# A two-layer decoder trunk in fp32 halves on one core: the weights' low halves all subtracted on VectorE, none on GpSimd, with a new issue order

## The chip, the cores and the metric

One core of one Trainium2 chip. The time is the device time of one execution in microseconds; the figure for a kernel is the median of its runs. TensorE (PE) multiplies, VectorE (DVE), ScalarE (ACT) and GpSimd (POOL) work on tiles in SBUF and PSUM, and SyncE (SP) issues the loads. Each engine takes its own instructions strictly in the order in which the program issues them.

## What is computed

Two decoder layers on 256 positions of width 1024, all in fp32. Per layer:

```python
h = rms_norm(x, pre_mix_norm[i]); z = h @ w_in[i]             # 1024 -> 2560, four head groups
out_a = block attention; out_b = gMLP spatial gating
out_c = conformer convolution (31 taps, depthwise); out_d = differential attention
x = x + rms_norm(concat(out_a, out_b, out_c, out_d) @ w_out[i], post_mix_norm[i])
x = x + rms_norm(gated conv FFN(rms_norm(x)), post_ffn_norm[i])  # up 1024 -> 5632, down 2816 -> 1024
x = x + sigmoid(rms_norm(x) @ w_pe_gate[i]) * (p[i] @ w_pe_proj[i])
```

## The kernel before, in words

**Weights in halves.** A matmul of fp32 accuracy is made of three in a reduced format (`mm3`): high times high, high times low, low times high. So each weight needs a rounded high part and the rest. All weights are packed into pieces of 128 x 2048 and loaded as halves of 128 x 1024, numbered k = 0 to 207 in the order of use (`PIECES`, `need`). `prep(k)` (line 303) gives each half three tiles of one ring of 25 (`TAGS`, tag `wt`): `raw` (512 KB, loaded by SP), `hi` (a rounding copy on ScalarE) and `lo` (raw minus hi). Which engine subtracts is read from a list, `POOL` (line 32), of 68 of the 206 halves that go through `prep`:

```python
nc.scalar.activation(hi, raw, AF.Copy)
eng = nc.gpsimd if k in POOL else nc.vector
eng.tensor_tensor(lo, raw, hi.bitcast(F32), op=ALU.subtract)
```

Both inputs of this subtraction lie in SBUF. The two halves of the first piece are made from four smaller loads (`rq`, `hq`, `lq`).

**The stages.** A layer is a mixer (`mixer`, line 483), a feed-forward part (`ffn`, line 889) and a gate. In the mixer TensorE projects `ca`, `cg`, `b`, `dk`, `dq`, `v`, `ak`, `aq`; VectorE rotates the queries and keys (`rot_*`), adds 60 convolution taps (`cacc`, one input in PSUM), makes the scaled, masked scores and their minima (`ed`, `ea`), layer norms (`gv`, `bl_ln`), the lambda of the differential attention (`lam_j`) and the low parts of each group's output (`cat_lo`); ScalarE makes exponentials and the high parts. Each group's output is then multiplied by its rows of `w_out` into the four tiles `y000` to `y011`. After the post norm the transposed rows become `hf_hi` and `hf_lo`. In the feed-forward part 22 tiles `u` are made by 48 matmuls each, each passing through VectorE (`u`, `uc`, `f`) and ScalarE, and 22 steps of the down projection (`f000` to `f011`) take them up. GpSimd also makes small reciprocal roots (`*_v`, `*_r`), masks and constants.

**The order of the work.** The program first records all operations (`Prog.record`), then issues them in the order that a long string, `ORDER` (line 1075), spells out (`Prog.issue`, line 190). A token is the engine's letter (t, v, s, g; s also stands for the loads of SyncE) and the tile: `v.lo20` is the subtraction of half 20 on VectorE, `t.dq0*28` the next 28 matmuls into `dq0`, `v.cacc0@5` the sixth tap. A tile gets a place of its ring when it is first issued, and gives it back after its last use. The string had been made by a planner outside the kernel. At the start TensorE runs 28 transposes that nothing uses (`busy`, `WARM`).

Of the kernel before, what the change touches and what calls it, by code (L numbers as in the profile page):

```python
# [1075 lines left out]
g.nhalf g.mask g.ident s.xt1 g.ident t.busy*2 g.ones t.busy*15 s.gc s.h0_hi@2 s.xt0 s.h0_hi@1 s.h0_hi*2 s.xt3 s.rq3  # L1076
s.rq0 g.mask s.xt2 s.rq2 v.h0_lo@1 s.posi s.h0_hi@6 v.h0_lo v.h0_lo@3 v.h0_lo@6 s.h0_hi@7 s.hq3 s.fr s.hq0 s.raw4
v.h0_lo v.h0_lo@7 v.lq3 v.lq0 s.h0_hi@5 v.h0_lo@5 t.busy s.rq1 t.ca0 s.h0_hi v.h0_lo s.raw2 s.hq2 v.lq2 s.hi4 s.xs
g.posf s.hq1 g.ang@2 s.hi2 s.xs@2*2 s.xs s.raw5 s.raw3 s.raw7 s.cols0 s.raw8 s.raw6 s.raw13 s.raw26 s.x10_s t.ca0*9
t.busy*8 t.ca0*4 t.busy*2 t.b00 v.lo4 t.b00*2 s.raw32 s.raw11 v.lq1 t.b00 t.ca0*24 s.raw9 s.raw10 t.ca0 t.cg0*2  # L1080
t.ca0*9 g.ang g.kf@2 g.kf v.lo2 g.kf s.x00_s s.x11_s g.n01_v s.x01_s g.n00_v g.n01_r g.n00_r s.hi5 t.cg0 g.kf t.cg0*3
s.hi3 v.lo3 t.cg0*22 v.lo5 s.mr0_d t.mr0 s.mr0_d s.hi7 t.mr0 t.cg0*6 v.ang@4 v.ang v.ang@5 t.cg0 v.ang t.cg0*7 s.hi8
t.cg0*6 t.b00*2 v.ang@6 s.mr0 v.ca0 v.cg0 s.hi6 g.cols0*2 v.lo6 t.b00*6 v.ang@7 v.ang s.cth g.ang@3 s.sin_d v.cg0
v.lo7 s.cacc0@1 s.cacc0 s.cos_d*2 s.hi9 t.b00*7 t.b01*10 t.b00*3 s.pt0 t.b00 s.raw20 s.raw17 s.raw12 v.ang s.hi13
g.ang s.raw14 s.raw19 v.cacc0@1 v.cacc0 s.chalf t.b00 g.lo8 s.raw29 s.gv s.raw15 s.raw24 v.cacc0@3 v.cacc0 v.cacc0@5
v.cacc0 v.cacc0@7 v.cacc0 v.cacc0@9 v.cacc0 v.cacc0@11 g.cos_d v.cacc0 s.gu v.cacc0@13 v.cacc0 v.cacc0@15 v.cacc0
t.b01*7 s.hi10 t.b01*5 s.raw18 t.b01*2 s.gu t.dk0*6 g.lo9 t.dk0*14 s.gv t.dk0*28 t.dq0 g.lo10 t.dq0*19 s.hi11 g.lo11
s.hi12 g.lo12 s.hi14 g.lo13 s.raw16 s.ph0 s.sin_a t.dq0*4 s.hi17 v.cacc0@17 v.cacc0 v.cacc0@19 v.tab_d0 v.cacc0@21
v.tab_d0 v.cacc0@23 v.cacc0 v.cacc0@25 s.hi19 v.cacc0 v.cacc0@27 v.cacc0 v.cacc0@29 v.rot_dk0 v.cacc0@31 v.dk0
v.cacc0@33 v.dk0 v.bl01_st t.dq0*23 v.cacc0 v.cacc0@35 v.rot_dk0 s.cos_a*2 s.hi16 s.hi29 s.first v.cacc0 v.bl01_mv  # L1090
g.lo14 t.dq0 v.rot_dq0 v.cacc0 v.dq0 v.cacc0 v.dq0 s.hi15 v.cacc0@37 v.cacc0 v.rot_dq0 t.v00*18 t.sc013 t.sc011
t.sc002 t.sc013 v.cacc0 v.bl00_st v.cacc0@39 g.bl01_v g.lo17 g.lo15 g.bl01_r v.bl00_mv v.ed03@2 t.sc011 s.sd1_0@6
v.ed01@3 t.sc002 v.ed02@1 s.raw27 v.ed02 v.ed03@3 s.sd1_0@7 t.v01*2 v.cacc0 t.v01*5 s.sd0_0@3 g.bl00_v v.ed01@2
v.cacc0 v.cacc0@41 v.cacc0 v.cacc0@43 t.v01*3 v.cacc0 t.sc001 t.sc010 t.sc003 t.sc010 t.sc003 s.raw28 v.ed03 v.cacc0
t.sc001 v.ed01@1 v.ed01 t.v01 t.v00*6 t.v01*2 s.hi27 t.v01*4 t.sc012 s.hi28 s.raw23 v.ed03 s.hi23 s.vsb00 g.lo16
t.sc000 t.sc012 t.sc000 g.bl00_r v.cacc0@46 v.cacc0 s.sd0_0@2 v.ed00@2 v.cacc0@48 s.hi18 s.sd1_0@2 v.ed00@3 s.sd1_0@1
s.sd1_0@4 s.sd1_0@3 s.sd1_0 t.v01*6 s.sd1_0 t.v01 v.lo19 s.rows0 v.lam_w v.gv*2 v.lam_w s.lam_w s.vsb01 v.bl0_ln*2
s.sd0_0@4 v.ed00 t.ak0 s.sd0_0 g.cos_a t.ak0*5 v.rd1_0@1 t.ak0*7 v.rd1_0 t.ak0*13 s.raw21 v.cacc0@50 v.cacc0
v.tab_a0@1 v.tab_a0 g.lo18 v.ed00 s.hi24 v.ed02 s.sd0_0 v.ed02 t.bm0*3 s.sd0_0@6 s.sd0_0*2 v.nlam0 t.bm0 v.bo v.cacc0
v.bo v.cd0 s.hi20 v.cd0 s.hi21 v.ed02 v.ed02@6*2 v.ed00@6 v.ed00 s.raw45 v.ed00*2 t.ak0*5 s.br00_s t.ak0 t.aq0*2  # L1100
t.ak0*3 v.ed02 t.ak0*2 t.aq0*15 s.g_post_mix0 t.aq0*3 t.ak0*11 t.wd00_pt s.br01_s t.aq0 t.wd00_pt*2 t.aq0*2 v.cacc0@52
t.aq0*3 s.hi26 t.aq0*5 s.raw22 v.rd0_0 v.rot_ak0 v.cacc0 v.ak0 v.cacc0@54 g.br00_v g.br01_v s.wd00_ps g.br00_r
s.br00_o t.wd00_pt t.aq0 t.wd00_pt g.br01_r t.wd00_pt s.br01_o s.od0*2 v.ak0 t.bt0*3 s.raw25 t.bt0 t.aq0*3 g.gsub0
t.aq0*13 t.wd03_pt*3 v.cacc0 v.rot_ak0 s.cat0_hi@1 s.cat0_hi v.cat0_lo*2 v.rot_aq0 v.rd0_0 v.aq0 v.cacc0@56 v.aq0
g.lo20 t.y000*3 t.wd02_pt*3 s.hi22 t.y000 s.wd03_ps t.wd03_pt*3 s.wd02_ps t.y001 t.wd02_pt*3 v.cacc0 v.rot_aq0 v.cacc0
s.od0@7 v.cacc0 s.od0@6 s.od0@4 g.lo21 g.lo26 t.y001 t.wd01_pt s.hi32 t.y001*2 t.y000*2 s.od0@5 t.wd01_pt*2 s.wd01_ps
t.sca03 v.cacc0 t.sca00*2 v.ea00 t.sca03 t.ct0*2 v.ea00 t.ct0*2 v.cst@1 v.cmv@1 g.cl01_v s.sa0*2 v.ea03@1 v.ra0 v.cst
v.cmv v.ea03 t.wd01_pt*3 s.od0@3 s.od0 g.cl01_r t.y011 v.cnm@1 t.y011*5 g.cl00_v g.cl00_r t.wa00_pt*3 t.y001*2 s.odsq
v.odss t.sca01 v.cnm s.wa00_ps t.sca02 t.sca01 v.ea01 t.sca02 g.odv g.odr t.wa00_pt*3 s.cn@1 v.ea02 s.cn t.csT0 v.ea02
t.csT0*2 s.oa0@1 s.oa0 v.ea01 t.csT0 s.cth2@1 s.cth2 s.cs t.y010*2 s.cs v.od0 v.cs*2 v.lo22 t.y010*4 t.pj001 t.pj010  # L1110
s.sa0@4 t.dt0*4 s.cat0_hi@3 t.cp0*4 v.co@1 v.co s.cat0_hi t.y010 t.y011 t.y000*2 s.sa0@6 v.cat0_lo@3 s.sa0@5 t.y011
s.raw36 v.cat0_lo v.ra0@2 s.sa0*3 s.cr00_s g.cr00_v t.wa03_pt*2 v.ra0@3 t.wa03_pt s.wa03_ps s.cr01_s t.y001*3 v.ra0
t.wa02_pt*3 s.wa02_ps t.y010 t.wa03_pt*3 t.y000*2 g.cr00_r g.cr01_v g.cr01_r v.lo23 s.oa0*2 s.cr00_o t.wa02_pt*3
v.lo27 t.wa01_pt*3 t.y011*2 t.y010*2 s.cr01_o s.wa01_ps t.wa01_pt*2 s.oa0@5 s.oa0 t.wa01_pt s.oa0 s.ar00_s g.ar00_v
g.ar00_r t.y001 t.y010 t.ctt0*4 s.oa0 s.cat0_hi v.cat0_lo s.ar01_s g.ar01_v t.y011 g.ar01_r t.y000*2 t.y001 t.y011
t.y001*2 t.y000 t.y001*2 t.y000 s.cat0_hi v.cat0_lo s.ar00_o v.lo28 s.raw30 v.pl0 s.raw33 t.y001 t.at0 v.lo29 t.y001
s.ar01_o t.at0 s.raw31 t.at0*2 s.cat0_hi*2 t.y010*3 s.raw47 s.hi30 s.raw39 t.y000*2 s.hi25 v.cat0_lo t.y001 t.y000*3
v.cat0_lo v.lo24 t.y000 t.y001 v.lo32 t.y001*5 s.pm001_s t.y000*4 s.pm000_s g.pm00_v g.pm00_r t.y010 t.y011*12 s.hi33
s.hi31 v.y000 v.xs t.nf00_t@1 t.nf00_t s.pm00x0_s v.y001 v.xs s.hf0_hi v.hf0_lo t.y010 s.pm011_s t.y010*4 t.pj001
s.hf0_hi g.lo25 v.hf0_lo s.raw42 t.y010 s.pm00x1_s v.y011 g.nf00_v s.raw37 t.nf00_t s.hf0_hi t.y010 v.hf0_lo t.y010*2  # L1120
t.nf00_t t.pj001*3 s.hf0_hi v.hf0_lo s.pm010_s t.pj001 s.proj001 t.nf00_t s.hf0_hi t.nf00_t s.hf0_hi t.pj010*5
s.proj010 v.y010 t.pj011*2 v.hf0_lo t.nf00_t s.hf0_hi g.nf00_r v.hf0_lo t.nf00_t t.pj011*3 s.hf0_hi t.pj000 g.pm01_v
g.pm01_r v.xs s.pm01x0_s v.hf0_lo*2 t.nf01_t s.hf0_hi v.hf0_lo t.pj011 t.nf01_t t.pj000*4 g.lo30 s.hf0_hi v.hf0_lo
s.proj011 t.nf01_t t.pj000 t.nf01_t t.u00*6 s.hf0_hi t.u00 v.xs v.hf0_lo s.hf0_hi v.hf0_lo s.proj000 t.nf01_t t.u00
g.lo31 t.nf01_t s.hf0_hi v.hf0_lo s.hf0_hi v.hf0_lo s.pm01x1_s s.qr0_d t.u00*3 t.u01*5 g.nf01_v t.u01 t.nf01_t
s.hf0_hi v.hf0_lo t.nf01_t s.hf0_hi s.hi36 s.hi39 s.raw38 v.hf0_lo s.hi38 g.nf01_r s.qr0_d v.lo33 v.lo36 s.raw34
s.hi34 t.u00*29 t.u01 t.u00*2 t.u01 t.qr0*2 t.u00*6 s.raw43 s.raw48 s.raw51 v.lo39 s.qr0 s.hi43 g.lo34 t.u01*4 s.raw35
t.u01*8 v.u00 s.uc0*2 s.raw49 t.u01*10 v.uc0@1 t.u01 v.uc0@3 v.uc0*2 s.raw40 s.hi37 g.lo37 s.uc0 s.raw44 t.u01*17
v.u01 t.u02*5 s.hi51 t.u02*23 v.lo38 s.uc1@1 v.uc0 s.uc1 v.uc1*3 s.hi47 v.uc1 s.hi44 v.lo44 t.u02*13 s.hi42 t.u02*6
t.u03*5 t.u02 t.u03*11 v.u02 s.uc2 g.lo42 v.uc2 v.uc2@2 s.uc2 v.uc2*2 s.hi45 t.u03*11 v.lo45 t.u03*21 s.f0 s.raw55  # L1130
# [192 lines left out]
```

## Time and profile before

| | us |
|---|---|
| median of 3 runs | 662.68 (662.63, 662.68, 665.95) |
| the profiled execution | 666.75 |
| its span, first to last instruction | 665.0 |
| TensorE busy | 645.8 |
| VectorE busy | 498.3 |
| ScalarE busy | 429.3 |
| GpSimd busy | 218.3 |

The span is the time from the first to the last instruction on the core; the execution's own time has 1.75 us more around it. An engine's busy time is the time in which it ran at least one instruction; the rest it waited, for another engine, for a load, or for nothing that is recorded. All operations stand under one source line (L230), since one function issues them, so the tile's name tells them apart. In a row of a timeline the first number is the start, the second the time taken by the instructions merged in it, and a bracket says how long the engine had been idle before it and for what.

### The profile page before, as it was taken

The numbers are of one execution on the slowest core, as the hardware profiler recorded it, in microseconds if no ns is written. First come the engines' busy times: TensorE is split into PE (matmuls) and PEld (weight loads), VectorE is DVE, ScalarE is ACT, GpSimd is POOL, SyncE is SP. The second block draws the span as 40 slices with busy tenths as digits, with TensorE's granted clock in tenths as the row PEclk, the third lists the DMA queues.
The fourth block names the chain that finished last, engine by engine and source line by source line (L and its number), as shares of the span: only waits on it lengthen the run. The fifth ranks groups of instructions, "written<-read, shape, count | busy, mean of one in ns | idle before, by whom it ended". The sixth has DMA issues, their size and how long they took to land.

```text
span 665.0 us, 11616 instructions
## 1 busy us (share of the span) xinstructions
PE 645.8 (97%) x4308; PEld 584.1 (88%) x4308; DVE 498.3 (75%) x974; ACT 429.3 (65%) x832; POOL 218.3 (33%) x179
## 2 busy tenths in 40 slices
...
GB/s 291 408 283 157 129 153 118 249 112 161 279 222 153 165 190 206 203 142 231 132 126 257 124 191 127 75 274 159 127 222 129 165 294 158 138 157 197 113 14 64
DMA packets 34040, 117.96 MB, mean 177 GB/s; under 512 B 4032, under 2 KB 4416, under 8 KB 33984
## 3 DMA queue, kind: packets, MB, share of 16 engines
...
HBM read 116.16 MB, written 1.05 MB: 176 GB/s over the span
## 4 chain that ended last, share of the span: by engine, by line
PE 84%; DVE 8%; ACT 4%; DMA 2%; issue 1%; POOL 1%; SPq 0%; DVEq 0%; ACTq 0%
PE u L230 32%; PE f L230 18%; PE gt L230 7%; PE y L230 6%; PE v L230 3%; PE b L230 3%; PE ca L230 2%; DVE lo L230 2%; PE cg L230 2%; DMA raw<-in_wpk_dram 2%; PE pj L230 2%; PE aq L230 1%; DVE uc L230 1%; ACT hi L230 1%; PE wd_pt L230 1%; DVE cacc L230 1%
## 5 line engine op out<-in xcount | busy, mean ns | idle before, releaser
L230 POOL TENSOR_TENSOR lo<-raw,hi 128x1024 fp32r<-128x1024 f32 x68 | 165.0, 2437 | 265.9 <-ACT hi L230 161.9
L230 ACT ACTIVATE hi<-raw 128x1024 fp32r<-128x1024 f32 x206 | 212.3, 1054 | 58.0 <-DMA raw<-in_wpk_dram 20.5
L230 PE MATMUL u<-hf_hi,hi 128*128 128x256 f32 x704 | 197.2, 282 | 2.5 <-ACT hi L230 1.7
L230 PE MATMUL u<-hf_lo,hi 128*128 128x256 f32 x704 | 197.4, 281 | 0.0
L230 PE MATMUL u<-hf_hi,lo 128*128 128x256 f32 x704 | 196.6, 281 | 0.0
L230 DVE TENSOR_TENSOR lo<-raw,hi 128x1024 fp32r<-128x1024 f32 x138 | 178.6, 1309 | 20.3 <-ACT hi L230 11.8
L230 PEld LDWEIGHTS u<-hf_hi,hi 128*128 128x128 f32 x704 | 132.4, 189 | 4.6 <-ACT hi L230 1.9
L230 PEld LDWEIGHTS u<-hf_lo,hi 128*128 128x128 f32 x704 | 132.6, 188 | 1.3
L230 PEld LDWEIGHTS u<-hf_hi,lo 128*128 128x128 f32 x704 | 132.4, 189 | 0.7
L230 PE MATMUL f<-hi,f 128*128 128x512 f32 x352 | 113.0, 395 | 0.0
L230 DVE SCALAR_TENSOR_TENSOR uc<-u,cols,uc 128x255 f32<-128x255 f32 (+1 forms) x176 | 80.3, 479 | 32.8 <-ACT uc L230 30.6
L230 ACT ACTIVATE uc<-u,cols 128x256 f32<-128x256 f32 x88 | 46.8, 560 | 68.3 <-DVE u L230 56.2
L230 PEld LDWEIGHTS f<-hi,f 128*128 128x128 f32 x352 | 65.6, 188 | 13.3
L230 PE MATMUL f<-lo,f 128*128 128x512 f32 x176 | 69.0, 395 | 0.0
L230 DVE TENSOR_TENSOR u<-u,qr 128x512 f32<-128x512 f32 x44 | 30.6, 695 | 28.4 <-PE u L230 28.3
L230 DVE SCALAR_TENSOR_TENSOR cacc<-cg,cols,cacc 128x254 f32<-128x254 f32 (+29 forms) x120 | 49.2, 458 | 0.9 <-ACT cacc L230 0.8
L230 PEld LDWEIGHTS f<-lo,f 128*128 128x128 f32 x176 | 33.1, 188 | 6.4
L230 ACT ACTIVATE uc<-uc 128x256 f32<-128x256 f32 x44 | 17.7, 411 | 18.1 <-DVE uc L230 18.1
L230 PE MATMUL gt<-hi,g_hi 128*128 128x512 f32 (+1 forms) x72 | 27.3, 384 | 0.0
L230 PE MATMUL gt<-lo,g_hi 128*128 128x512 f32 (+1 forms) x72 | 26.5, 377 | 0.0
L230 PE MATMUL gt<-hi,g_lo 128*128 128x512 f32 (+1 forms) x72 | 26.0, 375 | 0.0
L230 PE MATMUL y<-hi,cat_hi 128*128 128x512 f32 x64 | 25.6, 418 | 0.0
...
## 6 DMA issues: line engine op xcount, KB each, us to landing
raw<-in_wpk_dram SPq DMA_DIRECT2D x206, 512.0 KB, 4.7
...
```

The costliest lines, as they stand in the source:

```text
L230: getattr(getattr(tc.nc, o.eng), o.fn)(*[real(a) for a in o.args], **{k: real(v) for k, v in o.kw.items()})
```

## The change

The list `POOL` becomes empty, so that all 206 `lo` are made on VectorE, and the whole `ORDER` string is replaced (229 lines by 203). Nothing else changes: same operations, same tile shapes, same rings. All 68 `lo` of the list move from GpSimd's queue to VectorE's, and the tokens of every engine and of the loads stand in a new order. Of the 28 warm-up transposes, 12 now stand in `dq0` and `v00` and 4 just ahead of `b01`; before, all stood ahead of the first matmul of `b00`. Below are the list, and of the new string the stretch from `v.lo8` to `v.lo21` (mixer of layer 0) and that from `v.ca1` to the last `v.rot_aq1` (mixer of layer 1).

```diff
-POOL = (8, 9, 10, 11, 12, 13, 14, 15, 16, 17, 18, 20, 21, 25, 26, 30, 31, 34, 37, 40, 42, 43, 51, 57, 61, 62, 68, 92,
-        97, 101, 108, 114, 116, 117, 118, 120, 121, 122, 123, 124, 125, 126, 129, 131, 132, 134, 136, 137, 140, 142,
-        143, 145, 146, 148, 149, 153, 157, 160, 164, 168, 170, 172, 175, 183, 200, 203, 204, 206)
+POOL = ()
...
 ORDER = """
...
+t.busy*4 s.hi7 v.lo7 t.b01*6 s.cth v.cg0 s.cacc0@1 v.lo8 s.cacc0 v.cacc0*2 t.b01*2 s.chalf v.lo12 t.b01*3 v.cacc0@3
+t.b00 t.b01*2 s.raw15 t.b01*3 g.ang@3 g.ang g.gsub0 t.b00*5 s.raw11 s.rows0 s.raw21 s.hi20 s.raw14 v.cacc0 s.cos_d
+v.cacc0@5 s.raw17 v.cacc0 v.cacc0@7 v.cacc0 v.cacc0@9 v.cacc0 v.cacc0@11 v.cacc0 v.cacc0@13 v.cacc0 s.cos_a*2
+v.cacc0@15 v.cacc0 v.cacc0@17 v.cacc0 s.sin_a v.cacc0@19 t.b01*5 v.cacc0 s.cos_d g.cos_d v.tab_d0 t.b00 t.b01*3 s.gv@1
+t.b00*3 v.cacc0@21 s.gu@1 s.raw10 v.cacc0 s.hi10 t.b00*8 s.pt0 t.b00 v.bl01_st t.b00*5 s.gu s.gv v.cacc0@23 g.cols0
+v.cacc0 v.bl00_st v.cacc0@25 v.bl00_mv v.lo10 v.bl01_mv s.hi11 v.lo11 t.dk0 g.bl00_v t.dk0*14 g.bl01_v g.bl01_r
+g.cos_a t.dk0*18 g.bl00_r t.dk0*2 s.hi21 s.sin_d v.tab_d0 t.dk0*13 t.dq0*28 t.busy*5 v.rot_dk0 t.dq0*6 s.raw19 s.hi19
+t.dq0*14 s.raw18 s.hi18 s.raw13 s.hi13 v.cacc0 v.dk0 v.cacc0@27 v.cacc0 v.cacc0@29 v.cacc0 t.busy*2 v.dk0 v.lo13
+v.rot_dk0 t.busy s.raw45 t.v00*3 v.rot_dq0 t.busy*4 s.raw22 v.lam_w v.dq0 v.cacc0@31 v.dq0 v.gv@1 s.hi14 t.v00*7
+v.rot_dq0 t.v00*2 v.lo14 v.cacc0@33 v.lo19 s.raw23 t.sc002 t.sc000 t.sc013 t.v01*5 t.sc013 t.sc002 s.first v.ed02@1
+t.v01*6 v.cacc0 v.lam_w t.v01*2 v.cacc0 v.cacc0@35 v.ed03@3 v.ed03@2 v.ed02 t.v01 s.hi15 t.sc011*2 t.sc001*2
+v.cacc0@37 v.lo15 s.sd1_0@7 s.raw24 v.cacc0 v.cacc0@39 v.cacc0 t.sc000 t.v01*5 s.lam_w v.nlam0 v.ed00@1 s.raw29 s.hi29
+t.v01*3 t.v00*12 v.ed01@1 v.ed01@3 v.gv v.bl0_ln@1 v.bl0_ln t.bm0*2 v.ed01 s.sd0_0@2 v.cacc0 s.raw16 v.ed00 s.hi16
+v.lo16 s.hi17 v.ed01 t.sc003*2 s.hi23 v.cacc0@41 v.cacc0 v.cacc0@43 t.sc012*2 t.sc010 v.lo17 t.sc010 v.ed00@3 v.cacc0
+v.cacc0@45 v.cacc0 s.hi22 v.ed03@1 v.cacc0@47 v.cacc0 t.bm0*2 s.vsb00 t.ak0 s.raw31 t.ak0*6 v.cacc0@49 t.v01*2 s.vsb01
+t.ak0*8 v.ed02 t.ak0*9 s.sd1_0@6 t.ak0*5 s.raw26 t.ak0 s.sd1_0@5 t.ak0 s.sd1_0@4 v.rd1_0@1 v.tab_a0 v.ed03 v.bo
+s.sd1_0 v.lo18 t.ak0*4 s.hi26 t.ak0 v.ed00 v.ed02 t.ak0*5 s.raw32 s.sd1_0 s.sd1_0@3 s.sd1_0 v.rd1_0 s.sd0_0@1
+s.sd0_0@7 v.lo20 v.bo s.sd0_0@4 s.sd0_0 s.sd0_0@5*2 v.tab_a0 s.raw28 v.cacc0@51 s.sd0_0 v.cd0@1 v.cd0 v.rd0_0@1
+v.ed02@7 v.ed00 v.ed02 v.ed02@6 v.ed00@7 s.br01_s t.ak0*2 v.rd0_0 t.ak0*5 t.aq0*18 s.br00_s v.cacc0 t.aq0*3 s.raw33
+t.aq0*26 v.ed00 t.aq0 v.ed00 v.cacc0 v.cacc0@53 v.cacc0 v.rot_ak0 t.wd00_pt s.hi31 t.wd00_pt*2 s.wd00_ps t.wd03_pt*3
+s.wd03_ps t.wd00_pt g.br01_v g.br01_r t.wd00_pt*2 s.od0 v.cacc0@55 t.wd03_pt*3 s.od0 v.ak0 s.od0@7 s.od0@6 t.wd02_pt*3
+g.br00_v g.br00_r s.br01_o s.br00_o t.bt0*3 s.wd02_ps t.bt0 s.cat0_hi t.wd02_pt v.cacc0 s.cat0_hi s.raw25 v.rot_aq0
+t.y011 v.cacc0@57 s.hi24 v.ak0 v.aq0 t.wd02_pt*2 s.od0@5 v.cat0_lo v.aq0 t.y000*2 v.ed02 v.cat0_lo t.y000 v.rot_aq0
+v.cacc0 t.y001*3 t.wd01_pt*3 v.rot_ak0 s.hi28 s.od0@4 v.cacc0 s.wd01_ps t.y011*3 t.wd01_pt*3 s.od0 v.cacc0 v.lo21
...
+s.cth v.lo118 v.ca1 v.cg1 s.hi114 v.lo114 s.cacc1@1 s.cacc1 t.b11*16 s.gv s.raw122 s.gu t.dq1*4 s.raw131 s.hi131
+s.raw148 t.dk1*15 v.cacc1*10 t.dq1 v.cacc1 v.bl11_st v.cacc1 v.bl11_mv v.cacc1*3 v.gv v.cacc1@16 v.cacc1 v.cacc1@18
+v.cacc1 v.cacc1@20 v.cacc1 v.cacc1@22 v.cacc1 v.cacc1@24 v.cacc1 g.bl11_v t.dq1*3 s.raw116 s.hi116 t.dk1*2 s.hi122
+t.dk1*23 g.bl10_v g.bl10_r t.dk1*8 g.bl11_r v.bl1_ln@1 s.raw123 v.rot_dk1 s.raw126 s.raw120 v.lo116 s.raw121 v.cacc1*3
+v.dk1 v.bl1_ln t.dq1*12 s.raw125 s.hi120 t.dq1*17 v.dk1 s.hi121 t.dq1*11 v.rot_dq1 v.rot_dk1 v.dq1 v.cacc1@29 v.dq1
+t.bm1*4 t.v10*4 v.cacc1@31 t.v10*5 s.raw132 t.v10*6 v.rot_dq1 v.cacc1 v.lo122 t.sc102 t.sc113 t.sc101 t.sc102 t.sc101
+s.hi126 v.bo t.sc113 v.ed13@3 t.v11*5 v.ed12 v.ed13@2 t.v11 s.hi123 v.ed12 v.cacc1@33 v.ed11 v.bo s.sd0_1@2 s.br11_s
+s.raw128 t.sc100 t.sc103 t.sc100 t.sc103 v.ed13*2 s.br10_s v.ed10@1 s.sd1_1@2 s.sd0_1@1 v.lo120 v.cacc1@35 v.cacc1
+s.sd1_1@3 v.cacc1@37 v.cacc1 v.ed10 v.ed11 v.cacc1 s.hi128 s.sd1_1@6 t.v11 g.br11_v g.br11_r g.gsub1 s.br11_o t.v11*15
+g.br10_v t.v11*2 g.br10_r s.br10_o v.cacc1@39 v.cacc1 v.cacc1@41 s.vsb11 s.sd0_1 s.sd1_1@1 v.cacc1 v.cacc1@43 v.cacc1
+v.cacc1@45 v.cacc1 t.v10*9 s.vsb10 t.sc112 t.sc110 t.sc111*2 s.hi125 v.ed11 t.sc112 v.ed12@3 t.sc110 v.ed10@3
+s.sd0_1@5 v.lo125 s.sd0_1@7 t.bt1*2 t.aq1*6 t.bt1 v.lo121 t.bt1 s.cat1_hi@1 v.cat1_lo@1 t.ak1*16 s.sd1_1@4 t.ak1 t.aq1
+t.ak1*2 v.ed11 s.sd1_1@7 s.lam_w v.nlam1 t.ak1*28 s.raw134 t.aq1*5 s.raw127 t.aq1*3 t.ak1 v.cacc1@47 v.lo123 v.ed10
+s.raw130 s.sd0_1 s.sd1_1@5 s.sd1_1 v.rd1_1*2 v.rd0_1 v.cd1 v.ed12 v.ed12@5 v.ed12 v.cacc1@49 v.ed10 t.aq1*7
+t.wd11_pt*2 s.hi130 s.sd0_1 v.cacc1 s.cat1_hi v.cat1_lo s.g_post_mix1 s.sd0_1 s.raw124 v.cd1 v.ed10 s.hi124 t.wd10_pt
+t.wd11_pt s.hi127 v.cacc1 s.wd11_ps v.cacc1@51 t.wd10_pt*2 s.raw149 v.cacc1 v.ed12 t.aq1*5 t.wd11_pt*2 s.wd10_ps
+t.wd10_pt t.wd11_pt s.od1@2 t.wd10_pt*2 t.aq1*2 v.ed12 t.y111 t.aq1*2 s.od1@3 t.wd13_pt v.cacc1 t.aq1 v.cacc1@53
+v.cacc1 v.cacc1@55 v.cacc1 v.cacc1@57 t.wd13_pt v.cacc1 t.wd13_pt t.aq1*3 v.cacc1@59 t.aq1*2 v.cacc1 s.od1@1 t.aq1*6
+s.wd13_ps t.wd13_pt v.rd0_1 v.ed10@7 s.od1 t.wd13_pt*2 s.hi132 s.od1@7 t.ct1*3 t.y101 s.od1@6 v.ed10 t.ct1 s.raw133
+s.hi133 v.lo124 t.aq1*4 v.cst@3 t.aq1 v.cst t.wd12_pt*3 t.y111 v.rot_ak1 v.cmv@3 t.y111 s.wd12_ps t.wd12_pt*3 v.cmv
+t.y111*2 v.ak1 g.cl10_v t.y100*5 t.y101 t.y100 s.od1*2 s.odsq v.rot_aq1 v.odss t.y101*2 t.y111 t.y101*2 g.cl11_v
+g.cl10_r v.cnm s.cn t.csT1 v.aq1 g.cl11_r v.cnm s.cn v.ak1 v.aq1 v.rot_ak1 t.csT1*3 s.cth2*2 t.y110*2 s.cs t.y110*2
+s.cs t.y110*2 v.rot_aq1 t.sca10 t.sca11 g.odv g.odr v.od1 v.cs t.sca10 v.cs t.sca11 v.ea11*2 v.ea10 t.dt1*4
...
```

## Rows read from the trace of the kernel before

**Rows 1.** The page: busy time, share of the span and instructions of each engine.
```profile
PE 645.8 (97%) x4308; PEld 584.1 (88%) x4308; DVE 498.3 (75%) x974; ACT 429.3 (65%) x832; POOL 218.3 (33%) x179
```

**Rows 2.** Waits of PE: who waited for whom, us in total, times, longest.
```profile
PE bm L230 <- DVE bl_ln L230: 2.7, 1, 2.7
...
PE u L230 <- ACT hi L230: 1.7, 1, 1.7
PE ng_t L230 <- DVE g_lo L230: 1.2, 1, 1.2
```

**Rows 3.** Costliest groups: count, busy us, mean ns, idle before and its releaser.
```profile
L230 POOL TENSOR_TENSOR lo<-raw,hi 128x1024 fp32r<-128x1024 f32 x68 | 165.0, 2437 | 265.9 <-ACT hi L230 161.9
...
L230 DVE TENSOR_TENSOR lo<-raw,hi 128x1024 fp32r<-128x1024 f32 x138 | 178.6, 1309 | 20.3 <-ACT hi L230 11.8
```

**Rows 4.** Single tiles on DVE: ns min/median/max, first and last start, forms.
```profile
L230 DVE TENSOR_TENSOR lo<-raw,hi x138: 1202/1218/3428, 12.8 to 631.4; 128x1024 fp32r<-128x1024 f32 x138
...
L230 DVE SCALAR_TENSOR_TENSOR lam_j<-rows x4: 177/190/2396, 61.5 to 191.5; 128x32 f32<-128x32 f32 x4
...
L230 DVE SCALAR_TENSOR_TENSOR bl_ln<-gv,bl_r,rows x4: 471/475/2675, 64.8 to 368.1; 128x256 f32<-128x256 f32 x4
...
L230 DVE SCALAR_TENSOR_TENSOR cacc<-cg,cols,cacc x120: 418/458/484, 31.2 to 400.7; 128x255 f32<-128x255 f32 x4, 128x254 f32<-128x254 f32 x4, 128x253 f32<-128x253 f32 x4, 128x252 f32<-128x252 f32 x4
```

**Rows 5.** Windows, both mixers: length, busy us (instructions), clock, DMA share, GB/s.
```profile
31.20:81.90 50.70, 50.36 (x352) 44.68 (x352) 49.49 (x149) 42.42 (x89) 38.07 (x26) 1.00 0.55 202
351.50:407.80 56.30, 53.65 (x365) 48.03 (x365) 50.11 (x145) 34.43 (x78) 35.82 (x26) 0.97 0.57 193
```

**Rows 6.** The same windows, tile `lo` alone (PE, PEld, DVE, POOL).
```profile
31.20:81.90 50.70, 29.23 (x92) 17.21 (x91) 1.22 (x1) 33.66 (x14) 1.00 0.55 202
351.50:407.80 56.30, 29.73 (x94) 17.75 (x93) 0.00 (x0) 29.91 (x13) 0.97 0.57 193
```

**Rows 7.** Timeline of DVE, at 29 and at 94 us.
```profile
29.15 0.69 DVE L230 SCALAR_TENSOR_TENSOR cg<-cth,ca 128x512 f32<-128x512 f32 x1
...
93.88 2.34 DVE L230 TENSOR_TENSOR lo<-raw,hi 128x1024 fp32r<-128x1024 f32 x2
```

**Rows 8.** Timeline of PE, 82 to 85 us.
```profile
82.77 0.38 PE L230 MATMUL ct<-ident,cacc 128*128 128x128 f32 x2
...
84.12 0.39 PE L230 MATMUL y<-hi,cat_lo 128*128 128x512 f32 x1
```

**Rows 9.** Timeline of DVE and POOL at the stop of 368 us.
```profile
368.07 2.67 DVE L230 SCALAR_TENSOR_TENSOR bl_ln<-gv,bl_r,rows 128x256 f32<-128x256 f32 x1
368.12 7.20 POOL L230 TENSOR_TENSOR lo<-raw,hi 128x1024 fp32r<-128x1024 f32 x3 [2.45 <-PE dq L230]
```

**Rows 10.** Windows, the stretch after that stop (PE, PEld, DVE, ACT, POOL, PEclk).
```profile
371.00:374.50 3.50, 3.50 (x13) 3.06 (x13) 3.50 (x10) 0.54 (x1) 3.50 (x2) 0.52 0.47 152
```

**Rows 11.** Timelines of DVE and PE at 501 to 509 and 631 to 635 us.
```profile
501.66 3.43 DVE L230 TENSOR_TENSOR lo<-raw,hi 128x1024 fp32r<-128x1024 f32 x1
...
508.72 0.36 PE L230 MATMUL u<-hf_hi,hi 128*128 128x256 f32 x1 [1.67 <-ACT hi L230]
...
631.39 2.91 DVE L230 TENSOR_TENSOR lo<-raw,hi 128x1024 fp32r<-128x1024 f32 x1 [0.34 <-ACT hi L230]
...
634.62 0.33 PE L230 MATMUL ng_t<-ident,xs 128*128 128x128 f32 x1 [1.18 <-DVE g_lo L230]
```

**Rows 12.** Windows, feed-forward stages: all engines, then tile `lo` alone (PE, PEld, DVE, POOL).
```profile
120.00:300.00 180.00, 179.75 (x1297) 169.33 (x1297) 138.32 (x223) 108.75 (x173) 29.25 (x15) 1.00 0.57 192
...
440.00:620.00 180.00, 177.78 (x1287) 167.49 (x1286) 136.40 (x212) 109.60 (x174) 47.22 (x23) 1.00 0.55 184
...
120.00:300.00 180.00, 127.45 (x430) 80.25 (x430) 68.04 (x56) 27.88 (x12) 1.00 0.57 192
...
440.00:620.00 180.00, 124.50 (x424) 79.36 (x425) 66.49 (x47) 45.49 (x19) 1.00 0.55 184
```

**Rows 13.** Waits of DVE: us in total, times, longest.
```profile
DVE u L230 <- PE u L230: 28.3, 19, 3.7
```

385 lines of the change are left out of this document (156 added, 229 removed).

## The prediction

> **What bounds the kernel now.** First the busy times of the page: TensorE is busy for 645.8 of 665.0 us, VectorE for 498.3, GpSimd for 218.3 [rows 1]. The matrix instructions are the same before and after, so the time can move only by what TensorE waits; at most some 19 us are to be had, and there is no floor to what may be lost. Second the waits of TensorE: after the start, the long ones are 2.7 us for `bl_ln` of VectorE, 1.7 us behind a `hi` of ScalarE, 1.2 us for `g_lo` of VectorE [rows 2]. Third the costliest groups: every 128x1024 weight half becomes `hi` on ScalarE and `lo`, of which GpSimd makes 68 at 2437 ns and VectorE 138 at a mean of 1309 ns [rows 3]. VectorE's mean is above its own 1218 ns for an undisturbed one. What stretches it stands in the tiles' own views: `lam_j`, whose inputs are both in SBUF, has a median of 190 ns and once took 2396; `bl_ln`, also two SBUF inputs, 475 and once 2675; `cacc`, one of whose inputs is a PSUM tile, ran 120 times, beside many GpSimd `lo`, and never took over 484 [rows 4]. So a VectorE instruction with two SBUF inputs stands still while GpSimd subtracts, and one with a PSUM input doesn't notice.
>
> That agrees with the Trainium skill, "SBUF — State Buffer", "Who interferes with whom": an instruction of VectorE with two SBUF inputs and one of GpSimd that reads SBUF shut each other out, and issue order decides which waits. By that rule alone all the stretch goes with the change, which is the rival called "all stalls come back" below.
>
> **Part 1: 68 subtractions move to VectorE.** Added: two `lo` back to back took 2.34 us, so each costs 2.34 - 1.22 = 1.12 us of VectorE's time [rows 7]; 68 x 1.12 = 76 us. Removed: the stretch, 178.6 - 138 x 1.218 = 10.5 us on `lo` itself [rows 3], 2.2 on `lam_j`, 2.2 on `bl_ln` [rows 4]. VectorE goes from 498 to about 560 us of some 665, 84%. An average says nothing; the stages do.
>
> *Mixer of layer 0.* From the first convolution tap at 31.2 us to the last `rot_aq0`/tap at 81.9 us VectorE was busy 49.49 of 50.7 us, with one `lo` of its own (1.22 us), while GpSimd made 14, for 33.7 us [rows 5, 6]. This stage is VectorE's already, with GpSimd as the relief. In the new order VectorE's queue from `v.lo8` to `v.lo21` holds the same 125 other operations, neither more nor fewer, and 13 `lo` (8, 12, 10, 11, 13, 14, 19, 15 to 18, 20, 21) for the one. Without a gap that is 49.5 - 2.2 (the stretch of `lam_j`) + 12 x 1.12 = 60.7 us. It starts where the last multiply of `cg` ends, before at 29.15 + 0.69 = 29.8 us [rows 7], and the new queue puts nothing else between; so `lo21` ends at 90.5 us, and with half the 1.2 us of idle time that the stretch had, at 91.1. TensorE needs `lo21` for its second `y001` matmul. Ahead of that its new queue holds the matmuls that the kernel before had issued by 84.1 us, but for eight of some 480 [rows 8]. **Loss: 91.1 - 84.1 = 7.0 us.** Nothing covers it: the up-projection needs this mixer's output, and the same queue also delays `cat0_lo`, `od0` and `cs`, all in order behind it. Bounds: 4.0 if the chain begins 2 us earlier (the two range reductions that stood between are now done before) and the steps fall to 1.05 us; 9.0 if VectorE idles 1.2 us as before and one spell at the half clock is not hidden. Such a spell is seen once: after the stop of 2.65 us at 368 us (56.30 - 53.65 us of TensorE in [rows 5], behind `bl_ln`) the granted clock was 0.52 for 3.5 us, near the lower of its two levels (1.2 GHz of 2.4) [rows 9, 10], which costs 3.5 x 0.48 = 1.7 us.
>
> What else moves here: 12 of the 28 warm-up transposes (`busy`) go from the start into `dq0` and `v00`, where TensorE waits for `lo10` to `lo15`; they are hidden by that wait, and cost at most 12 x 0.19 = 2.3 us if it isn't there (two transposes of this size, `ct`, took 0.38 us together) [rows 8]. SP's queue is shuffled: half 2 now comes ahead of two first-piece loads, halves 9 and 12 ahead of the 0.6 MB of `cols0`. The DMA engines were busy for 0.55 of this stage [rows 5], so I give the shuffle nothing, with 1 us either way in the bounds.
>
> *Mixer of layer 1.* From 351.5 to 407.8 us VectorE was busy 50.1 of 56.3 us with no `lo` at all, GpSimd made 13 [rows 5, 6]. The new queue has 8 there (114, 116, 122, 120, 125, 121, 123, 124); the others are made before it. 50.1 - 2.2 (the stretch of `bl_ln`) + 8 x 1.12 = 56.9 us, with 1 us of idle 57.9: 1.6 us more than before. Against it, six more `y` matmuls stand ahead of `sca10` than before, 1.4 us of TensorE's work that is then done. The stop of 2.65 us and the half clock [rows 9, 10] are already in the 56.3. **Net 0**, between -4.3 (stop and half clock gone, VectorE hidden) and +3 (idle time as before).
>
> *Feed-forward stages.* VectorE was busy 138.3 of 180 us in layer 0 (120 to 300 us) and 136.4 in layer 1 (440 to 620), and GpSimd's share was 12 and 19 `lo` [rows 12]. Added 12 x 1.12 and 19 x 1.12, less the stretch in layer 1 (66.5 - 47 x 1.218 = 9.2 us): 152 and 148 of 180, under TensorE's 180. Their cover is that slack of 28 us; it counts only if a `lo` isn't stuck behind a `u` multiply that waits for TensorE, a wait that VectorE meets for 28.3 us in all [rows 13], and past which GpSimd went freely. **0**, bounds 0 and +4.
>
> **Part 2: stops that the stretch made.** Of the three long waits after the start, that at 368 us is counted above. At 501.66 us a `lo` of VectorE took 3.43 us beside one of GpSimd, and TensorE, served by the work queued behind it, stood idle for 1.67 us ahead of its matmul at 508.72. At 631.39 a `lo` took 2.91 us, `g_lo` came after it, and `ng_t` waited 1.18 us [rows 11]. **Gain 2.85 us** if the new order has no such place; bounds 0 and 2.85.
>
> **The sum** against the profiled execution's own time: 666.75 + 7.0 + 0 + 0 - 2.85 = 670.9 us. The runs' median is 662.68, 4.07 below the profiled one, and one run (665.95) is as long as it. These 4 us are of the size of the stops that the stretch makes, so the median runs may lack some of them; then there is less to win back. I count half of the 2.85: 662.68 + 7.0 - 1.4 = 668.3, **668 us**.
>
> A rule speaks on this point: the Trainium skill, "Perfetto Trace Analysis", "Optimizing Scalar/DVE Operations", says that where VectorE is saturated, offloading some work to GpSimd may make sense, but may not help because the two share a port. The trace shows the first half in the mixer of layer 0: 33.7 us of GpSimd's work cost VectorE 2.2 us there [rows 4, 6]. By the second half of the rule the first mixer would lose nothing and the sum would be 661.3.
>
> **The rivals.** 0.5% (3.3 us: below 659.4 or above 666.0) is about what a measurement of this kernel can tell from no change.
> - *First mixer slower, forecast.* For it: 98% busy VectorE in [rows 5] and 12 more `lo` in its queue. Against: the start of the chain is mine, by one row. 668 us, 665.5 to 671.5. Chance 0.47 for its part above 666.0.
> - *The loss is given back*, no change: the stop at 368 with its half clock (4.3 us) goes as well as the 2.85. 662.7 + 7.0 - 4.3 - 1.4 = 664. For it: `bl_ln` takes 0.48 us instead of 2.68. Against: 8 `lo` in that same queue. 0.26, with the small results of the forecast.
> - *All stalls come back*, faster: one mechanism, that GpSimd's hold on the shared inputs is what sets the stops, and the first mixer's chain starts 2 us earlier. 662.7 + 4.0 - 4.3 - 2.85 - 1.0 (many waits too small for a row) = 658.5. It decides if `lo21` ends before 88 us and no `bm1` stop is left. Against: 12 `lo` of 1.12 us in a stage with 1.2 us of room. 0.16.
> - *The feed-forward queue breaks*, slower still: a `lo` in VectorE's one queue stands behind a `u` multiply, TensorE waits as ahead of 508.72, 1.67 us a time. At five of the 44 `u` tiles 668 + 8.4 = 676; it decides from two on. For it: 56 + 12 and 47 + 19 `lo` in queues that already wait. Against: 28 us of slack. 0.11.
> That GpSimd makes no `lo` any more can't fail: the list is empty.
>
> **The numbers.** Slower 0.47 + 0.11 = 0.58; same 0.26; faster 0.16. Low end: 662.7 + 4.0 - 4.3 - 2.85 = 659.5, taken to 659 for the rival below it; high end: 662.7 + 9 + 1 (DMA) + 4 = 676.7, taken to 677. The forecast's own range is 665.5 to 671.5.
>
> **What would show it.** Right: `lo21` ends at 90 to 93 us; VectorE over 98% busy from 30 to 90 us; TensorE's idle time between 25 and 91 us up by some 7 us; no VectorE `lo` over 1.3 us; the waits behind 2.91 and 3.43 us `lo` gone; VectorE near 560 us in all. Wrong: `y001` issued by 86 us; TensorE idle in `u` between 120 and 300 us by over 3 us; a stop at `bm1` as long as before.

## The result and the profile after

| | before | after |
|---|---|---|
| median, runs shown | 662.68 us | 669.91 us (667.93, 669.91, 670.46) |
| ratio | 1 | 1.0096, 95% interval 1.0067 to 1.0125 |
| the profiled execution | 666.75 | 667.93 |
| its span | 665.0 | 666.2 |

Slower by about 1%. A second measurement, later and with more runs, gave 671.02 us (6 runs) and a ratio of 1.0112 (1.0082 to 1.0142). The page of after, busy times and the group of `lo`, against [rows 1, 3]:

```profile
PE 645.4 (97%) x4308; PEld 582.5 (87%) x4308; DVE 554.7 (83%) x1042; ACT 428.0 (64%) x832; POOL 60.4 (9%) x111
...
L228 DVE TENSOR_TENSOR lo<-raw,hi 128x1024 fp32r<-128x1024 f32 x206 | 247.9, 1217 | 23.4 <-ACT hi L228 19.6
```

TensorE does the same work in the same busy time; VectorE has 56 us more, GpSimd 158 less. The single tiles of after (ns min/median/max, as in [rows 4]):

```profile
L228 DVE TENSOR_TENSOR lo<-raw,hi x206: 1186/1217/1227, 11.7 to 647.4; 128x1024 fp32r<-128x1024 f32 x103
...
L228 DVE SCALAR_TENSOR_TENSOR bl_ln<-gv,bl_r,rows x4: 468/474/483, 63.3 to 377.4; 128x256 f32<-128x256 f32 x4
...
L228 DVE SCALAR_TENSOR_TENSOR lam_j<-rows x4: 178/180/183, 51.6 to 169.4; 128x32 f32<-128x32 f32 x4
```

The stretch is gone to the last instruction: no `lo` over 1.23 us (3.43 before), no `bl_ln` over 0.48 (2.67). The long waits that it made are gone from TensorE's list as well, and others stand there, against [rows 2] (the first two are at the start, ahead of the last `cg`):

```profile
PE ca L228 <- ACT hq L228: 7.5, 1, 7.5
PE cg L228 <- ACT hi L228: 1.6, 1, 1.6
...
PE n_t L228 <- DVE h_lo L228: 1.5, 1, 1.5
PE bt L228 <- ACT br_o L228: 0.9, 1, 0.9
```

So every stall that was to come back came back, and the kernel is slower all the same. Where the time is lost is read at five points of TensorE's queue: the last matmul of `cg` in layer 0, the first `u` of layer 0, the last `f` of layer 0, the first `u` of layer 1, the last `gt`. At the second, fourth and fifth the same work lies behind it in both kernels. At the first, before has done 4 matmuls of `b` and 16 warm-up transposes more, which after does in the first mixer (0.9 and 1.6 us, each matmul counted from its start to the next one's); at the third it has done one `gt` less. In the timeline of after these points, and what the prediction was about, are:

```profile
27.11 0.28 PE L228 MATMUL cg<-h_hi,lo 128*128 128x256 f32 x1
...
89.84 1.21 DVE L228 TENSOR_TENSOR lo<-raw,hi 128x1024 fp32r<-128x1024 f32 x1
...
91.21 0.48 PE L228 MATMUL sca<-rot_ak,rot_aq 64*128 64x128 f32 x2
91.62 0.50 PE L228 MATMUL y<-hi,cat_hi 128*128 128x512 f32 x1
91.96 0.39 PE L228 MATMUL y<-lo,cat_hi 128*128 128x512 f32 x1
...
127.86 0.28 PE L228 MATMUL u<-hf_hi,hi 128*128 128x256 f32 x1
...
340.44 2.02 ACT L228 ACTIVATE hi<-raw 128x1024 fp32r<-128x1024 f32 x2 [2.80 <-DMA raw<-in_wpk_dram]
...
343.81 0.34 DVE L228 SCALAR_TENSOR_TENSOR h_lo<-n_t,gc,h_hi 128x128 fp32r<-128x128 f32 x1
...
344.21 0.33 PE L228 MATMUL n_t<-ident,xs 128*128 128x128 f32 x1 [1.46 <-DVE h_lo L228]
...
450.33 0.36 PE L228 MATMUL u<-hf_hi,hi 128*128 128x256 f32 x1
...
661.59 0.28 PE L228 MATMUL gt<-hi,g_lo 128*128 128x256 f32 x1
```

The `lo` at 89.84 is half 21, and the matmul at 91.96 is the first that reads it. The same points read from the other profiles give the stages (us; differences of such starts, the last column up to the end of the span; "before again" is a second profile of the kernel before, 662.52 us, and "after again" one of after, 672.4 us):

| kernel | to last `cg` | to first `u` 0 | to last `f` 0 | to first `u` 1 | to last `gt` | to the end |
|---|---|---|---|---|---|---|
| before | 26.42 | 93.44 | 187.88 | 134.83 | 215.69 | 6.74 |
| before again | 26.45 | 93.37 | 187.88 | 130.63 | 215.69 | 6.78 |
| after | 27.11 | 100.75 | 187.83 | 134.64 | 211.26 | 4.61 |
| after again | 28.14 | 100.79 | 188.21 | 137.29 | 211.61 | 4.66 |

Against "before again", after loses 0.7 and 1.7 us at the start, 7.4 and 7.4 in the first mixer, nothing in the first feed-forward part, 4.0 and 6.7 in the gate and the second mixer; it wins 4.4 and 4.1 after that and 2.2 and 2.1 behind the last matmul. That is 5.4 and 9.9 us, the whole difference of the spans (660.8 to 666.2 and to 670.7).

One sign that the prediction named for itself did not come: TensorE's idle time between 25 and 91 us was to grow by some 7 us. It grew by 1.35, from 0.34 to 1.69 us. The windows from 25 to 91 us (length, busy us of PE, PEld, DVE, ACT and POOL, then clock, DMA share, GB/s) of before and of after:

```profile
25.00:91.00 66.00, 65.66 (x446) 57.40 (x445) 60.82 (x184) 54.11 (x115) 42.07 (x33) 1.00 0.55 205
```

```profile
25.00:91.00 66.00, 64.31 (x424) 55.92 (x423) 64.81 (x167) 45.66 (x95) 7.78 (x15) 1.00 0.56 198
```

TensorE counts as busy for nearly as long as before, and gets through 22 matmuls fewer.

### The profile page after: what moved, and what is told of

The parts are those of the page before. It is cut to its first block, busy times and chain, and to the rows that moved or that the text cites. A ratio compares the mean times of both kernels' runs of the same rounds, so it can differ in the third digit from the quotient of the medians.

```text
span 666.2 us, 11543 instructions
## 1 busy us (share of the span) xinstructions
PE 645.4 (97%) x4308; PEld 582.5 (87%) x4308; DVE 554.7 (83%) x1042; ACT 428.0 (64%) x832; POOL 60.4 (9%) x111
## 4 chain that ended last, share of the span: by engine, by line
PE 83%; DVE 8%; DMA 5%; ACT 3%; issue 1%; POOL 0%; SPq 0%; ACTq 0%; DVEq 0%; POOLq 0%
PE u L228 38%; PE f L228 18%; PE y L228 6%; PE gt L228 6%; DMA raw<-in_wpk_dram 4%; DVE cacc L228 3%; PE b L228 2%; PE pj L228 2%; DVE lo L228 2%; DVE ed L228 1%; PE cg L228 1%; PE v L228 1%; PE wd_pt L228 1%; PE ca L228 1%; PE dk L228 1%
## 5 line engine op out<-in xcount | busy, mean ns | idle before, releaser
L228 DVE TENSOR_TENSOR lo<-raw,hi 128x1024 fp32r<-128x1024 f32 x206 | 247.9, 1217 | 23.4 <-ACT hi L228 19.6
L228 DVE SCALAR_TENSOR_TENSOR cacc<-cg,cols,cacc 128x238 f32<-128x238 f32 (+27 forms) x120 | 48.4, 458 | 0.1
L228 ACT ACTIVATE f<-uc 128x256 fp32r<-128x256 f32 x44 | 17.5, 407 | 13.4 <-DVE uc L228 13.4
```

The source lines that it names most:

```text
L228: getattr(getattr(tc.nc, o.eng), o.fn)(*[real(a) for a in o.args], **{k: real(v) for k, v in o.kw.items()})
```

## Experiments

Ratios are against runs of the kernel before beside them (medians 662.36, 662.73 and 662.75 us in three sessions).

### List and order apart

`oldorder_none`: the old string, the new list. `neworder_pool`: the other way round.

```diff
# oldorder_none (in the string of before, for each of the 68)
-POOL = (8, 9, 10, ...
+POOL = ()
-g.lo20
+v.lo20
# neworder_pool (in the string of after, for each of the 68)
-POOL = ()
+POOL = (8, 9, 10, ...
-v.lo20
+g.lo20
```

> The order of before, but all 68 lo in VectorE's queue, each at its old place in the string. Theory 1 (VectorE's queue in the first mixer sets the loss): the 13 lo of the first mixer cost 13 x 1.12 - 2.2 = 12.4 us of VectorE's queue, of which about 1 us is room, and 11 to 13 lo of the second mixer cost some 10 more, with 6 of room and the stop at bm1 gone; 662.7 + 10 + 3 - 1.4, so 674 us (670 to 680), TensorE late by 7 to 11 us at the first u. Theory 2 (the new order costs the time, the list nothing): 659 to 663 us.

> The order of after, but the old list of 68 lo back in GpSimd's queue, each at its place in the new string. Theory 1: VectorE's queue in the first mixer is short again, so most of the 8 us goes, and stops from the stretch come back: 664 us (661 to 667), first u within 3 us of before. Theory 2 (the new order itself costs the time): 669 to 671 us, first u 6 to 8 us later than before.

Measured: 696.15 us (1.0497, 1.0482 to 1.0512) and 693.22 us (1.0458, 1.0427 to 1.0489). Neither theory had these: the list alone costs 34 us, the order alone 31, both together 7 to 8. They are two halves of one plan, and it makes no sense to ask which of them lost the time. Stages of `oldorder_none`: 112.02 us from `cg` to `u` (93.37), 335.88 from there to the second `u` (318.51), 216.10 to the last `gt` (215.69). My 10 us for the first mixer were 18.6, the 3 for all up to the second `u` were 17.4 (3.5 of them in the first feed-forward part, 13.8 in the gate and the second mixer), and the late gain didn't come at all: with the stretch gone TensorE waited elsewhere. Its waits:

```profile
PE v L228 <- DVE rot_dk L228: 5.2, 1, 5.2
PE bm L228 <- DVE bl_ln L228: 4.1, 1, 4.1
PE u L228 <- DVE uc L228: 3.7, 5, 1.2
...
PE y L228 <- DVE lo L228: 3.4, 1, 3.4
```

Each is something short that TensorE needs and that stands behind other work, `lo` among it, in VectorE's one queue. `neworder_pool` took 118.20 us from `cg` to `u`, 24.8 more than before.

`neworder_m0pool`: the new string, only the old list's 13 of the first mixer back on GpSimd.

```diff
-POOL = ()
+POOL = (8, 9, 10, 11, 12, 13, 14, 15, 16, 17, 18, 20, 21)
-v.lo20
+g.lo20
```

> The order of after, with only the 13 lo of the first mixer (halves 8 to 18, 20, 21) back in GpSimd's queue. Theory 1: lo21 ends near 82 to 86 us instead of 91, the first u comes 4 to 7 us earlier than in after, the time is 664 us (662 to 666), less than after by 4 to 7 us. Theory 2: no earlier than after, 669 to 671 us.

Measured: 681.36 us (1.0281, 1.0258 to 1.0304), 11 us worse than after where I expected 6 better. `cg` to `u` took 113.82 us. The timeline shows the price of GpSimd at places that were laid out for VectorE:

```profile
65.96 7.41 POOL L228 TENSOR_TENSOR lo<-raw,hi 128x1024 fp32r<-128x1024 f32 x3 [11.08 <-ACT hi L228]
66.03 2.62 DVE L228 SCALAR_TENSOR_TENSOR gv<-gv,bl_mv,rows 128x256 f32<-128x256 f32 x1
68.58 5.08 DVE L228 SCALAR_TENSOR_TENSOR bl_ln<-gv,bl_r,rows 128x256 f32<-128x256 f32 x2
...
73.71 1.23 PE L228 MATMUL bm<-bl_ln,cols 128*128 128x128 f32 x4 [3.54 <-DVE bl_ln L228]
```

Three short instructions of VectorE with two SBUF inputs (0.48 us alone) each last as long as one of GpSimd's three `lo`. The Trainium skill, "SBUF — State Buffer", "Who interferes with whom", says that the two shut each other out and that issue order decides which one waits. The trace agrees, and the price of one collision here is some 2.1 us, 2.6 for 0.48. This wait of 3.54 us is not the whole of the 13 us that the stage is longer than in after. Two more stretched instructions of VectorE (`lam_j` with 2.00 us at 52.93, `ed` with 2.58 at 90.27) come some us ahead of waits of TensorE of 1.7 and 1.1 us, though it isn't shown that they make these, and the granted clock is at 0.50 from 58.7 to 62.1, from 72.3 to 79.2 and from 96.2 to 103.1 us.

`old_ffn`: the old string, 44 `lo` outside the two mixers' stretches moved in place, 24 left.

```diff
-POOL = (8, 9, 10, ...
+POOL = (8, 9, 10, 11, 12, 13, 14, 15, 16, 17, 18, 20, 21, 114, 116, 117, 118, 120, 121, 122, 123, 124, 125, 126)
-g.lo25
+v.lo25
```

> The order and list of before, with only the 44 lo outside the two mixers' stretches (25 to 108 and 129 to 206) moved to VectorE's queue, in place; 24 stay with GpSimd. Theory 1 (28 us of slack in the feed-forward stages hide them, and the stretched lo at 501 and 631 us go): 661 us (659 to 663), no loss of TensorE in u over 1 us. Rival (a lo in VectorE's one queue stands behind a u multiply): 665 us or more, with stops of TensorE in u.

Measured: 673.39 us (1.0169, 1.0154 to 1.0184): the rival. Of the 11 us, 10.2 lie between the two first `u` (328.71 for 318.51): 3.5 in the first feed-forward part, 6.7 in the gate and the second mixer, where 6 of the 44 are made and the granted clock is at 0.50 for 3.4 us at 385.6. The second feed-forward part lost 0.7. Its waits of TensorE:

```profile
PE u L228 <- DVE uc L228: 3.7, 5, 1.2
...
PE nf_t L228 <- DVE hf_lo L228: 1.7, 2, 1.1
PE u L228 <- DVE lo L228: 1.6, 4, 0.7
```

The tile `lo` alone in the two feed-forward parts (PE, PEld, DVE, POOL) of "before again" and of this run:

```profile
119.82:307.70 187.88, 131.51 (x440) 82.14 (x440) 69.28 (x57) 30.82 (x14) 1.00 0.57 193
438.33:654.02 215.69, 144.31 (x480) 89.74 (x480) 69.69 (x50) 51.98 (x21) 1.00 0.46 155
```

```profile
121.34:312.74 191.40, 131.75 (x440) 82.16 (x440) 84.52 (x71) 0.00 (x0) 1.00 0.56 189
450.05:666.47 216.42, 144.53 (x480) 89.69 (x480) 85.38 (x71) 0.00 (x0) 1.00 0.45 152
```

So the slack covered most, but not all: 15.2 us more of VectorE's work cost 3.5 us in the first part, and 15.7 us cost 0.7 in the second, with the two late stops of 1.7 and 1.2 us gone there. For the rest the order has to put each `lo` where VectorE would wait anyway. The string of after does that: its first feed-forward part is as long as before's.

### Is the first mixer VectorE's?

`before_again` and `after_again` are the two kernels, unchanged.

> The kernel before, unchanged, for a second profile of it: its runs here are near 662.4 us, the profile shown was 666.75. If the 4 us between them are stops that the stretch makes (2.67 us at bl_ln with the half clock behind it, 1.67 at 508 us, 1.18 at 634), a profiled execution of 662 to 663 us lacks at least one of them and TensorE's idle time falls by 3 to 4 us; if not, the stops are all there and the difference lies elsewhere (start or end).

> The kernel after, unchanged, against the kernel before in more runs: 668 to 670.5 us, ratio 1.009 to 1.012; first u 127 to 128.5 us, lo21 ending at 90.5 to 91.5 us as in the first profile.

Measured: 662.52 us, and 671.02 us (in the second profile of after, `lo21` ended at 92.10 and the first `u` came at 128.93, each some 0.5 us later than expected). The second profile of before has these waits of TensorE:

```profile
PE u L230 <- ACT hi L230: 1.7, 1, 1.7
...
PE ng_t L230 <- DVE g_lo L230: 1.2, 1, 1.2
...
PE bm L230 <- DVE bl_ln L230: 0.4, 1, 0.4
```

The 4.2 us between the two profiles of before are the stop at `bm1` and the half clock behind it [rows 9, 10], 2.3 and 1.6 us, and little else; the late stops [rows 11] are there each time. Of the 46 runs of the kernel before in all, five took 666 to 668 us (665.95 the lowest of them), the others at most 664.6.

`dup4_m0`: four `lo` of the first mixer made twice. `omit13_m0`: 13 of them not made.

```diff
# dup4_m0, TWICE = (11, 14, 16, 20); the string has v.lo11*2 for v.lo11 and so on
-        eng.tensor_tensor(lo, raw, hi.bitcast(F32), op=ALU.subtract)
+        for _ in range(2 if k in TWICE else 1):
+            eng.tensor_tensor(lo, raw, hi.bitcast(F32), op=ALU.subtract)
# omit13_m0, NONE = (8, 10, 11, 12, 13, 14, 15, 16, 17, 18, 19, 20, 21); their tokens are left out
+        if k in NONE:
+            wt[k] = (hi, hi)
+            return
```

> The kernel after, with the lo of halves 11, 14, 16 and 20 (first mixer) subtracted twice, the second time over the first. Theory 1 (VectorE's queue sets this stage's end): lo21 and the first u come 4 x 1.12 = 4.5 us later (4 to 5.5), first u at 132 us, the time 674 us (673 to 676). Rival (the stage waits for loads, ScalarE or TensorE, and VectorE is busy beside it): first u later by under 2 us, time 670 us.

> The kernel after, with the 13 lo of halves 8 and 10 to 21 left out (their matmuls read hi in place of lo, so that their low part is not computed). Theory 1: VectorE has 14.5 us less to do in the first mixer, TensorE becomes the limit, the first u comes 6 to 8 us earlier, at 120 to 122 us, and the time is 662 us (660 to 664). Rival (order, loads or the start cost the time): first u within 3 us of after, 667 us or more.

Measured: 674.30 us (1.0163, 1.0130 to 1.0196) and 668.47 us (1.0069, 1.0044 to 1.0094). From `cg` to `u`: 106.09 us with four more `lo`, 100.86 with 13 fewer, 100.75 in after. The windows from 29.8 to 91.1 us (length, busy us of PE, PEld, DVE, ACT and POOL, then clock, DMA share, GB/s) of after and of the kernel without the 13:

```profile
29.80:91.10 61.30, 59.61 (x392) 51.55 (x390) 60.87 (x161) 43.15 (x92) 6.42 (x11) 1.00 0.53 181
```

```profile
29.80:91.10 61.30, 59.73 (x391) 52.24 (x389) 47.57 (x149) 42.03 (x91) 4.67 (x11) 0.97 0.51 191
...
86.00:88.00 2.00, 2.00 (x6) 1.48 (x5) 2.00 (x6) 1.57 (x4) 0.00 (x0) 0.50 0.00 0
88.00:90.00 2.00, 2.00 (x10) 1.75 (x9) 1.32 (x4) 0.49 (x1) 0.00 (x0) 0.64 0.00 0
```

What a spell costs is read from the distance between the starts of the same matmuls in two runs, ahead of the spell and behind it. Adding hurts nearly in full: 5.3 us, of which 1.5 is a spell at the lower clock at 72 to 76 us, the rest 3.8 of the 4.5 expected. VectorE's queue has under 1 us of room. But taking away gives little, though VectorE is now busy for only 47.57 of 61.3 us: the spell at 86 to 90 cost this run 1.3 us, and without it the stage would be 1.2 us shorter than in after, for 13.3 us less of VectorE's work. Theory 1 in its simple form falls. In the new order something else takes just as long as VectorE.

`omit13_busy0`: as `omit13_m0`, the 16 late transposes put back to the start.

```diff
-t.busy
+t.busy*17
...
-t.busy*4 s.hi7 v.lo7 t.b01*6
+s.hi7 v.lo7 t.b01*6
-t.dq0*28 t.busy*5 v.rot_dk0
+t.dq0*28 v.rot_dk0
```

> As the run that leaves out 13 lo of the first mixer (halves 8 and 10 to 21; their matmuls read hi), and the 16 late warm-up transposes moved back to the start. Theory (without those lo, TensorE's own queue is what holds this stage, so anything taken out of it shows in full): first u 1.3 to 1.8 us earlier than in that run (128.25), at 126.4 to 127.0 us. Rival (a chain through ScalarE, VectorE or the loads holds it, and the transposes fill its waits): within 0.5 us of 128.25.

Measured: 667.30 us (1.0084, 1.0047 to 1.0121), the first `u` at 127.53 for 128.56, between what the two theories allowed. From `cg` to `u` it took 98.91 us for 100.86. The same two matmuls ahead of the spell and behind it, in this run and in `omit13_m0`:

```profile
85.56 0.55 PE L229 MATMUL wd_pt<-vsb,wd_ps 128*128 128x64 f32 x4
89.44 0.92 PE L229 MATMUL sca<-rot_ak,rot_aq 64*128 64x256 f32 x6
```

```profile
85.30 0.55 PE L229 MATMUL wd_pt<-vsb,wd_ps 128*128 128x64 f32 x4
90.44 0.92 PE L229 MATMUL sca<-rot_ak,rot_aq 64*128 64x256 f32 x6
```

At the last `cg` this run is 0.92 us behind (28.62 for 27.70, all 28 transposes stand ahead), at `wd_pt` 0.26 behind, at `sca` 1.00 ahead. So 1.3 of the 1.95 us are the spell, which this run lacks there, and the 16 transposes cost some 0.7 us of the 1.4 that they take in the queue: they fill waits, as the prediction had it, by half. This is without the 13 `lo`; with them no run tried it.

What is left is TensorE's own queue with its round trips: without the 13 `lo` and without the transposes, the first mixer is still 5.5 us longer than in "before again" (98.91 for 93.37), and 0.9 of that is the four matmuls of `b`. Summed from each matmul's start to the next one's, up to the first `u`, the 36 `wd_pt` take 6.55 us in after and 3.34 in "before again", the 32 `sc` 4.08 and 2.57, the 16 `sca` 2.37 and 1.71; in `omit13_busy0` they take 6.30, 3.43 and 2.38, together 4.5 more than in "before again". These are the small steps of the attention, each behind a step of ScalarE or VectorE (`wd_ps`, `br_o`, `rot_dq`). Before, `aq` matmuls stood between them; in the new order `aq` is done first. That this is the reason, and which of them one could move, is not settled: no run tried another order of TensorE's queue there.

### The new stop at the second layer

`after_late119`: in after, ScalarE's `hi119` waits for its load, ahead of the `h_hi` that TensorE's `n_t` waits for (the rows at 340 to 344 us above).

```diff
-s.h1_hi s.hi119 s.hi105 v.h1_lo v.lo119 t.gt011*3
+s.h1_hi s.hi105 v.h1_lo t.gt011*3
...
-t.n11_t s.hi112 s.h1_hi s.gx010_s v.h1_lo t.b10*6
+t.n11_t s.hi112 s.h1_hi s.gx010_s v.h1_lo s.hi119 v.lo119 t.b10*6
```

> The kernel after, with hi119 and lo119 put behind two h_hi and h_lo of the next layer's norm, ahead of which they stand in after, where ScalarE waits 2.8 and 4.5 us for their load. Theory (this load sets the stop of TensorE ahead of n_t at 343 us, 1.5 us in one profile, 3.1 us and a spell at the half clock in the other): the stop is under 0.6 us, the time 667 us (666 to 668.5) with less spread. Rival (h_lo is late for another reason): the stop stays at 1.4 us or more, 669 to 671 us.

Measured: 670.01 us (1.0099, 1.0071 to 1.0128). The stop is down to 0.2 us, and the stage from last `f` to the second `u` takes 133.22 us (134.64 and 137.29). The median doesn't show it: in the profiled run the first mixer took 103.35 us, with this in its windows:

```profile
80.00:82.00 2.00, 1.62 (x14) 1.14 (x12) 2.00 (x8) 0.60 (x3) 0.69 (x2) 1.00 0.36 100
82.00:84.00 2.00, 2.00 (x15) 1.69 (x15) 2.00 (x7) 1.26 (x6) 0.00 (x0) 1.00 0.58 221
84.00:86.00 2.00, 1.09 (x7) 1.08 (x6) 2.00 (x7) 1.25 (x4) 0.00 (x0) 0.69 0.04 8
86.00:88.00 2.00, 1.76 (x9) 1.47 (x7) 1.66 (x4) 1.78 (x3) 0.00 (x0) 0.50 0.00 0
88.00:90.00 2.00, 2.00 (x6) 1.61 (x6) 2.00 (x6) 1.46 (x3) 0.00 (x0) 0.50 0.00 0
90.00:92.00 2.00, 2.00 (x8) 1.47 (x7) 2.00 (x4) 0.45 (x1) 0.00 (x0) 0.60 0.00 0
```

The cause of the stop is shown, its worth in the median isn't.

### A version faster than both

`before_stops`: the old string and list, but for three `lo` whose runs on GpSimd stand beside the stretched ones late in the kernel, and the stores at the end in the order in which their data is ready. `before_stops122` moves half 122 too.

```diff
-g.lo170
+v.lo170
-g.lo183
+v.lo183
-g.lo206
+v.lo206
-v.xs@22 t.gt110*14 s.gth t.gt111 v.gth t.gt111*2 s.xs@7 t.gt111 v.xs t.gt111*20 s.gth v.gth v.xs s.xs@8 s.xs s.xs@6 s.xs
+v.xs@22 s.xs@7 s.xs s.xs@6 t.gt110*14 s.gth t.gt111 v.gth t.gt111*3 v.xs s.xs t.gt111*20 s.gth v.gth v.xs s.xs
# before_stops122 also
-g.lo122
+v.lo122
```

> The kernel before, with only the lo of halves 170, 183 and 206 moved to VectorE, in place (they run beside the lo and uc that stand still at 497, 537 and 627 us), and the four last stores put in the order in which their data is ready. Theory: TensorE's stops of 1.9, 0.7 and 1.3 us go (gain 2 to 3.5 us), and the end after the last multiply falls from 5.0 us to some 3 (gain 1.5 to 2.5 us): 658 us (656.5 to 659.5), faster than both kernels. Rival (the stops return at the moved lo, and the stores are bound by their transfer): 661.5 to 663 us.

> As the run with halves 170, 183, 206 and the stores, and the lo of half 122 moved to VectorE too, behind bl_ln, beside which GpSimd runs it now. Theory: the stop at bm1 (0.4 to 2.7 us, with the half clock behind the long one) goes, for 1.1 us more in VectorE's queue with 6 us of room: 657.5 us (656 to 659), and no run 4 us above the others. Rival (the second mixer's VectorE queue is as tight as the first's): 1 us slower than without it.

Measured: 657.95 us (0.9933, 0.9909 to 0.9957), faster than both kernels, and 658.99 us (0.9939, 0.9918 to 0.9961). Both have 213.05 us from the second `u` to the last `gt` (2.6 less than before; after has 4.4 less), and 4.61 and 4.66 us behind it (6.78). VectorE's last multiply in `before_stops`, whose span is 659.5 us:

```profile
656.25 0.43 DVE L228 SCALAR_TENSOR_TENSOR xs<-gth,xs 128x256 f32<-128x256 f32 x1
```

From its end to the end of the span are 2.8 us, for 5.0 in "before again" (655.37 + 0.43 to 660.8): SP's queue held three finished stores behind the last one. With half 122 moved, both theory and rival came true in part: its runs lie between 658.2 and 659.7 us, while two of the seven without it took about 661 (the profiled one, 661.25, has a 2.7 us wait at `bm1`), but its median is 1 us longer. The two intervals overlap, so which is better is not settled.

## Why the prediction came out as it did

Forecast 668 us, slower; measured 669.9 and 671.0. The sign and the size of the largest term were right. That the sum came so near is in part luck: against the median run, terms put at nothing cost 4.7 and 8.4 us (the start, and the gate with the second mixer), and 5.2 and 4.8 us came back beyond the 1.4 that had been counted (late stops and the end).

- **First mixer, +7.0.** Measured +7.4 and +7.4 from `cg` to the first `u`, 0.9 of it the four matmuls of `b`. `lo21` ended at 89.84 + 1.21 = 91.05 us, for which 91.1 had been worked out, and VectorE was busy for 60.87 of 61.3 us. The count of the queue was right. The step that failed is "nothing covers it", with TensorE's own way to `y001` taken at 84.1 us from the kernel before: in the new order TensorE came there by itself, straight from `sca`, at 91.62, and at 91.96 to the matmul that reads `lo21`, 0.9 us after `lo21` was there. VectorE's queue and TensorE's queue tie, and the price is paid once; TensorE's idle time, which grew by 1.35 us and not by 7, fits that. Taking the 13 `lo` away returns some 1.2 us (`omit13_m0`), so that the size of this term fits is a coincidence of two queues.
- **Warm-up transposes, hidden.** Half right without the 13 `lo`: about 0.7 us of 1.4 showed (`omit13_busy0`). With them it was not measured.
- **Loads, nothing, 1 us either way.** `cg` ended 0.7 and 1.7 us later. Past the first mixer I gave SP's queue no term, and there one late load set the new stop of 1.46 us (3.1 us in the second profile, with a spell at a granted clock of 0.50 to 0.66).
- **Second mixer, net 0.** Right against the profile that it was worked out from, gate included (134.64 us for 134.83), mis-sized against the median run: 4.0 and 6.7 us lost. The base was [rows 5], with the stop at `bm1` in its 56.3 us. Most runs of the kernel before lack that stop, so the median had nothing there to give back. That was the term behind the rival "the loss is given back". Of the 4.0 us, 1.4 go with the new stop ahead of `n_t` (`after_late119`); the rest is open.
- **Feed-forward parts, 0.** Right for this order (187.83 and 188.21 us for 187.88). The slack alone would have left 3.5 us in the first part and 0.7 in the second (`old_ffn`); the order covers these.
- **Late stops, -2.85, half of it counted.** Measured -4.4 and -4.1. Halving was wrong: I took the 4 us between profile and median for late stops that median runs lack, and it was the stop at `bm1`. The late ones stand in each profile of before.
- **The end**, not in the sum: -2.2 and -2.1, from the order of the stores.
- **"All stalls come back".** They did, and VectorE is at 554.7 us for the 560 forecast; what the rival left out is that the room they leave is less than the work that takes their place. The rule of the Trainium skill, "Perfetto Trace Analysis", "Optimizing Scalar/DVE Operations", that offloading between these two may not help, holds for one order and not for the other: in the new one, 13 `lo` given back to GpSimd cost 11 us (`neworder_m0pool`); in the old one, the 68 on GpSimd are worth 34 us (`oldorder_none`).
